# One block inversion emitted between dense projection tiles, and a full-width transpose in place of two narrow ones

## Chip, cores and metric

The kernel runs on one core of a Trainium2 chip. The metric is the device time of one execution in microseconds (us); several executions give a median. The trace was taken from one profiled execution of the kernel before the change.

## What is computed

One step of a one-layer hybrid decoder over 512 prompt tokens and 32 sample tokens: a half-step feed-forward, a projection of the normalised activations, two groups of heads (sparse attention and RWKV-7), an output projection and a second feed-forward.

```python
xp = ffn_half(xp, ffn1_norm[l], ffn1_wg[l], ffn1_wu[l], ffn1_wd[l])
zp = rms_norm(xp, mix_norm[l]) @ w_in[l]
...
o_nsa_p, wk_p, wv_p = nsa_prompt(qp, kvp, gp, cmp_w, rel_bias_table)
o_rw_p, wkv_p, sh_p = rwkv_mix(zp[..., NSA_COLS:], ...)
...
xp = xp + jnp.concatenate([o_nsa_p, o_rw_p], axis=-1) @ w_out[l]
xp = ffn_half(xp, ffn2_norm[l], ffn2_wg[l], ffn2_wu[l], ffn2_wd[l])
```

The RWKV group has 8 heads of width 64 and a delta-rule state. The kernel computes it in chunks of 64 tokens, and each chunk of each head needs the inverse of a 64x64 unit triangular matrix. That inverse is the place of the change.

## The kernel before, in words

Activations live transposed: 128 features on the partitions, 544 token columns as two halves of 272. The projection of the mixing stage, `w_in`, is cut into 25 tiles of 128 output features. A tile is eight feature blocks of the input by three products (high by high, high by low, low by high part) by two halves: 48 dense matmuls of 128x272 on TensorE (PE), all issued from line 159 (`dense`) into a PSUM tile `acc`, of which there are two. The weights of half a tile come with one DMA from SyncE (`wraw`), ScalarE (ACT) makes the high part (`wh`, line 150) and VectorE (DVE) the low part (`wl`, line 152).

Tiles 0 to 13 belong to RWKV: two for all heads, then three (key, value, receptance: `xs_k`, `xs_v`, `xs_r`) for each of four head pairs 0 to 3. So pair 2 has tiles 8 to 10 and pair 3 has tiles 11 to 13. `rwkv_prep(si)` works on half `si`, that is on pairs 2si and 2si+1; for each pair:

- `shifted` turns a projection tile into a token-shifted row block (DVE lines 483 to 491, GpSimd 487 to 489, ACT 490);
- two small matmuls for decay and in-context rate go through sigmoid on ACT (lines 562 to 565), a scan on DVE (566), a matmul by `blk1` for a norm (line 497, called from 569), then a chain of ACT (571, 572, 576, 580, 581) and DVE work (570, 574 to 591) that ends in the operands `bk` and `ar`;
- 64 block products of `bk` and `ar` (line 598) make the matrices `L` (DVE masks them at 601), 64x64 transposes by matmul (607, 614) give `BK` and `UV` (ACT 610, 617), and a last matmul by `blk1` (line 497 again) feeds `gbs` and `orw` (DVE 627 to 629). PE line 598 to this last matmul is called the tail of a pair below.

These small products rotate through two PSUM banks, `pp`; those of the inversion and of the chain of chunks through two others, `pq`.

`rwkv_inverse(L)` inverts the triangles of one half, so the first one covers pairs 0 and 1. It has two parts. The diagonal part runs on DVE: three transposes of `L` into `A` (lines 636, 638; the last two have 32 partitions each), an elimination of 15 steps with two instructions each (653, 654), and two transposes of the result, `Dt` and `Dn` (656, 658). The product part runs on PE in four groups of tiny matmuls, each of which needs an evacuation of the group ahead: 664 (64 products of 16 columns), then ACT 666; 672 and 674 (96 products), then DVE 677 and ACT 679; 685 (32 products), then ACT 688; 693 (32 products), then ACT 696. GpSimd copies blocks into `L` (668).

Instructions are written in program order, but a scheduler puts those of each engine into their final order, and each engine then works through its row strictly in order; with `keep_in_program_order` a matmul stays behind what was written ahead of it. Before the change no product of the inversion is held like that.

Of the kernel before, what the change touches and what calls it, by code (L numbers as in the profile page):

```python
# [7 lines left out]
F32 = mybir.dt.float32  # L8
F32R = mybir.dt.float32r
I32 = mybir.dt.int32  # L10
AF = mybir.ActivationFunctionType
# [6 lines left out]
KT = 8  # L18
# [10 lines left out]
HW = 272  # L29
# [19 lines left out]
class Step:  # L49
# [301 lines left out]
    def mix(self):  # L351
        nc = self.nc
        r = self.norm_end()
        with ExitStack() as st:
            self.mc = self.pool("mc", 1, st)
            self.un = self.pool("un", 1, st)
            self.orw = self.mc.tile([128, 4, 2, HW], F32, name="orw")
            un1 = self.un1 = self.pool("u1", 1, st)
            with ExitStack() as s0:
                un0 = self.pool("u0", 1, s0, side="right")  # L360
                with ExitStack() as s2:
                    self.rwkv_setup(s2)
                    self.lanes = "p"
                    S0 = self.rwkv_prep(0, r, un0)
                    self.lanes = "q"
                    self.rwkv_inverse(S0[0])
                    self.lanes = "p"
                    S1 = self.rwkv_prep(1, r, un1)
                    nc.scalar.dma_start(self.O["sh"], self.sho.rearrange("p a b -> p (a b)"))
                self.lanes = "q"  # L370
                self.ch = self.pool("ch", 1, s0, side="right")
                self.rwkv_chain(0, un0, *S0)
                self.rwkv_inverse(S1[0])
            self.az = self.pool("az", 1, st, side="right")
# [90 lines left out]
    def mix_consts(self):  # L465
# [10 lines left out]
        nc.gpsimd.tensor_copy(self.id2[64:128], self.ident[64:128, 64:128])  # L476

    def shifted(self, i, col, r, tp, xs):
        nc = self.nc
        p = self.win_tile(i)  # L480
        z = tp.tile([128, ZW], F32, name="zp", tag="zp", bufs=2)
# [46 lines left out]
    def rwkv_prep(self, si, r, up):  # L528
        nc, I = self.nc, self.I
# [14 lines left out]
        ar = []  # L544
        pcp = up.tile([128, 2, 8], F32, name="pcp")
        L = up.tile([128, 2, 16, 128], F32, name="L")
        BK = up.tile([128, 2, 2, 8, 64], F32, name="BK")
        UV = up.tile([128, 2, 2, 8, 64], F32, name="UV")
        for pi in range(2):
            p = 2 * si + pi  # L550
            if p == 1:
                room = self.un1.tile([128, 7, ZW], F32, name="prep", tag="L")
                k, v, rr, sig, a, Lc, sq = (room[:, j] for j in range(7))
# [38 lines left out]
            for h in range(2):  # L592
                pl = [self.ps() for hh in range(2)]
                for cc in range(4):
                    c = 4 * h + cc
# [33 lines left out]
            nc.vector.tensor_mul(c64(self.orw[:, p, 1, SW:HW]), half(pb[1][:, :ZW - ZP[1][0]]), half(v[:, ZP[1][0]:ZW]))  # L629
        return L, BK, UV, ar, pcp  # L630

    def rwkv_inverse(self, L):
        nc, un = self.nc, self.un
        A = un.tile([128, 32, 32], F32, name="ivA", tag="iA")
        Lt = L.rearrange("p x c t -> p t (x c)")
        nc.vector.transpose(A, Lt[:, 0:32])
        for s in (slice(32, 64), slice(96, 128)):
            nc.vector.transpose(A[s], Lt[s, 32:64])
        N = un.tile([128, 32, 32], F32, name="ivN", tag="iN")
# [17 lines left out]
        Dn = un.tile([128, 32, 32], F32, name="ivDn", tag="iD")  # L657
        nc.vector.transpose(Dn.rearrange("p b t -> p t b"), N)
        grp = [(hh, q, 64 * hh + 32 * q) for q in range(2) for hh in range(2)]
        T = un.tile([128, 16, 16], F32, name="ivT", tag="iN")  # L660
        p = self.ps()
        for c in range(16):
            for hh, q, g in grp:
                nc.tensor.matmul(p[g:g + 32, c * 16:c * 16 + 16], L[g:g + 16, hh, c, 32 * q:32 * q + 32], Dt[g:g + 16, 16 * hh + c, 0:16],
                                 start=True, stop=True)
        nc.scalar.activation(T, p[:, 0:256].rearrange("p (c s) -> p c s", s=16), AF.Copy, scale=self.half)
        for hh, q, g in grp:
            nc.gpsimd.tensor_copy(L[g:g + 32, hh, :, 32 * q:32 * q + 32], Dn[g:g + 32, 16 * hh:16 * hh + 16])
        pt, pz = self.ps(), self.ps()
        for c in range(16):  # L670
            for hh, q, g in grp[0:2]:
                nc.tensor.matmul(pt[g:g + 32, c * 16:c * 16 + 16], Dn[g:g + 32, 16 * hh + c], T[g:g + 32, c], start=True, stop=True)
            for hh, q, g in grp:
                nc.tensor.matmul(pz[g:g + 16, c * 16:c * 16 + 16], T[g:g + 32, c], Dn[g:g + 32, 16 * hh + c, 16:32], start=True, stop=True)
        for hh, q, g in grp[0:2]:
# [6 lines left out]
        for c in range(16):  # L682
            for hh in range(2):
                g = 64 * hh
                nc.tensor.matmul(p[g + 32:g + 64, c * 32:c * 32 + 32], L[g:g + 32, hh, c, 32:64], Dt[g:g + 32, 16 * hh + c], start=True, stop=True)
        for hh in range(2):
# [3 lines left out]
        for c in range(16):  # L690
            for hh in range(2):
                g = 64 * hh
                nc.tensor.matmul(p[g:g + 32, c * 32:c * 32 + 32], W[g + 32:g + 64, c], L[g + 32:g + 64, hh, c, 32:64], start=True, stop=True)
        for hh in range(2):
            s = slice(64 * hh, 64 * hh + 32)
            nc.scalar.activation(L[s, hh, :, 32:64], p[s].rearrange("p (c t) -> p c t", t=32), AF.Copy)

    def rwkv_chain(self, si, up, L, BK, UV, ar, pcp):
# [933 lines left out]
```

## Time and profile before

| | us |
|---|---|
| median of 3 runs | 1522.66 (1521.82 to 1527.6) |
| profiled execution, whole | 1521.93 |
| profiled execution, span from first to last instruction | 1520.1 |
| TensorE busy in the span | 1367.9 |
| VectorE, ScalarE, GpSimd busy | 707.0, 512.1, 250.7 |
| mean granted TensorE clock | 0.929 |

Times in the rows are counted from the start of the span. Busy time of an engine counts overlapping instructions once. A tiny or small matmul on 32-bit operands leaves two records in the trace, a dense one leaves one. The granted clock is 1.00 at 2.4 GHz and 0.50 at 1.2 GHz.

### The profile page before, as it was taken

To read this page: it belongs to the slowest core of one execution; us is meant where nothing else is said; L and a number is where in the kernel's file an instruction comes from. 1 tells how busy PE (TensorE), PEld (TensorE's weight loads), DVE (VectorE), ACT (ScalarE), POOL (GpSimd) and SP (SyncE) were. 2 spreads that over 40 slices of the span, in tenths; PEclk is the share of its full clock that TensorE was granted. 3 is DMA by queue.
4 is the path that set the end of the run, shared out by engine and by line. 5 is a ranking of instruction groups with operands and counts; after the bars stand their busy time and mean duration, and the time that the engine had idled before them with its cause. 6 is when DMAs were issued, how large, how long until landed. Compare 5 with 4: busy or idle time off the path is not lost.

```text
span 1520.1 us, 31735 instructions
## 1 busy us (share of the span) xinstructions
PE 1367.9 (90%) x13337; PEld 1272.0 (84%) x13337; DVE 707.0 (47%) x1357; ACT 512.1 (34%) x928; POOL 250.7 (16%) x313
## 2 busy tenths in 40 slices
PE   9969686877799999889899986889999999999996
PEld 8969586766799999778776884567999999999996
DVE  6423222222333345694968764457454444443223
ACT  6212121121232236545222334457443333332321
POOL 2153332415100011212000223320100000000100
PEclk9979697978799999997999997889999999999998
DMA  4533333434334342111131564731532222233332
GB/s 158 186 121 102 94 104 107 139 112 139 94 103 119 114 129 86 43 43 39 37 110 29 171 182 149 215 112 44 175 103 89 87 91 86 89 91 106 109 105 84
DMA packets 99329, 163.25 MB, mean 107 GB/s; under 512 B 16186, under 2 KB 42882, under 8 KB 98547
## 3 DMA queue, kind: packets, MB, share of 16 engines
q1 hardware_dynamic: 74978, 116.10, 25.0%
q0 software_dynamic: 9040, 25.24, 5.6%
q10 hardware_dynamic: 15168, 19.89, 4.4%
q8 instruction: 105, 1.72, 0.5%
q14 instruction: 38, 0.30, 0.1%
HBM read 150.19 MB, written 16.72 MB: 110 GB/s over the span
## 4 chain that ended last, share of the span: by engine, by line
PE 80%; issue 7%; DVE 6%; ACT 3%; another core or an unknown queue 1%; DMA 1%; POOL 0%; ACTq 0%; DVEq 0%; SPq 0%; POOLq 0%
PE acc L159 63%; PE pS L969 1%; PE pq L972 1%; PE po L969 1%; PE pp L969 1%; PE pq L714 1%; PE pq L956 1%; PE pp L956 1%; DMA wraw<-in_wg 1%; PE pp L598 1%; PE pp L796 1%; PE pp L497 1%; PE pp L159 1%; DVE ivt L653 0%
## 5 line engine op out<-in xcount | busy, mean ns | idle before, releaser
L159 PE MATMUL acc<-hl,wh 128*128 128x272 f32 x2064 | 437.9, 296 | 27.5 <-issue 26.4
L150 ACT ACTIVATE wh<-wraw 128x512 fp32r<-128x512 f32 x338 | 209.7, 620 | 685.6 <-PE acc L159 507.1
L159 PE MATMUL acc<-hh,wh 128*128 128x272 f32 x1808 | 394.9, 298 | 33.2 <-issue 29.9
L159 PE MATMUL acc<-hh,wl 128*128 128x272 f32 x1808 | 391.8, 297 | 26.0 <-issue 24.4
L152 DVE TENSOR_TENSOR wl<-wraw,wh 128x512 fp32r<-128x512 f32 x338 | 232.5, 688 | 337.4 <-ACT wh L150 279.7
L159 PEld LDWEIGHTS acc<-hl,wh 128*128 128x128 f32 x2064 | 332.0, 194 | 41.0 <-issue 37.2
L159 PEld LDWEIGHTS acc<-hh,wh 128*128 128x128 f32 x1808 | 296.0, 194 | 42.1 <-issue 35.6
L159 PEld LDWEIGHTS acc<-hh,wl 128*128 128x128 f32 x1808 | 293.2, 194 | 33.5 <-issue 30.5
L918 POOL DMA_INDIRECT cp<-in_cmp,idx x128 | 125.0, 976 | 204.6 <-PE pp L956 80.3
L159 PE MATMUL acc<-ah,wh 128*128 128x272 f32 x660 | 137.0, 289 | 0.0
L159 PE MATMUL acc<-al,wh 128*128 128x272 f32 x660 | 136.2, 287 | 0.0
L159 PE MATMUL acc<-ah,wl 128*128 128x272 f32 x660 | 135.5, 286 | 0.0
L126 POOL TENSOR_TENSOR ss<-ss,sq 128x544 f32<-128x544 f32 x23 | 32.0, 1393 | 599.7 <-ACT sq L122 584.3
L159 PEld LDWEIGHTS acc<-al,wh 128*128 128x128 f32 x660 | 104.0, 188 | 0.0
L159 PEld LDWEIGHTS acc<-ah,wl 128*128 128x128 f32 x660 | 103.3, 188 | 0.0
L159 PEld LDWEIGHTS acc<-ah,wh 128*128 128x128 f32 x660 | 102.9, 188 | 0.0
L194 DVE TENSOR_TENSOR t<-acc,r 128x544 f32<-128x544 f32 x42 | 30.4, 724 | 111.3 <-PE acc L159 87.3
L196 DVE TENSOR_TENSOR u<-acc,r 128x544 f32<-128x544 f32 x42 | 30.4, 724 | 108.8 <-PE acc L159 78.5
L918 POOL DMA_INDIRECT kv<-in_slc,idx x36 | 35.5, 986 | 130.1 <-DVE Y L747 64.2
L199 ACT ACTIVATE ah<-u 128x544 fp32r<-128x544 f32 x44 | 29.0, 658 | 65.1 <-DVE u L197 59.3
L200 DVE TENSOR_TENSOR al<-u,ah 128x544 fp32r<-128x544 f32 x44 | 31.9, 725 | 29.0 <-ACT ah L199 28.3
L1416 ACT ACTIVATE ra<-pq 128x512 f32<-128x512 f32 (+2 forms) x48 | 23.7, 521 | 35.9 <-remote 15.4
(515 smaller groups left out, 1482.0 us busy)
## 6 DMA issues: line engine op xcount, KB each, us to landing
wraw<-in_wg SPq DMA_DIRECT2D x88, 256.0 KB
wraw<-in_wu SPq DMA_DIRECT2D x88, 256.0 KB
wraw<-in_wd SPq DMA_DIRECT2D x80, 256.0 KB
wraw<-in_win SPq DMA_DIRECT2D x50, 256.0 KB
kv<-in_slc SPq DMA_DIRECT2D x60, 128.0 KB
x<-xr ACTq DMA_DIRECT2D x16, 272.0 KB
xr<-x ACTq DMA_DIRECT2D x16, 272.0 KB
wraw<-in_wout SPq DMA_DIRECT2D x16, 256.0 KB
```

The costliest lines, as they stand in the source:

```text
L126: nc.gpsimd.tensor_add(self.ss, self.ss, sq)
L150: nc.scalar.activation(wh[:, :m], w[:, :m], AF.Copy)
L152: nc.vector.tensor_sub(wl[:, :m], w[:, :m], wh[:, :m].bitcast(F32))
L159: self.nc.tensor.matmul(p[h] if isinstance(p, list) else p[:, h, :HW], a, b[:, h], start=f, stop=l)
L194: nc.vector.tensor_mul(t, pt, r)
L196: nc.vector.tensor_mul(u, pu, r)
L199: nc.scalar.activation(ah[:, f], u, AF.Copy)
L200: nc.vector.tensor_sub(al[:, f], u, ah[:, f].bitcast(F32))
L918: self.nc.gpsimd.indirect_dma_start(out=tile[:, k], out_offset=None, in_=rows, in_offset=bass.IndirectOffsetOnAxis(ap=self.idx[:, k0 + k:k ...
L956: nc.tensor.matmul(ph[64 * x:64 * x + 64, 0:w], self.w1[:, x, j], self.cp[:, 0:w // 4, x, j], start=j == 0, stop=j == 31)
L969: self.tc.keep_in_program_order(self.nc.tensor.matmul(*args, **kw))
L1416: self.nc.scalar.activation(t[:, 0:o + w], p[:, 0:o + w], AF.Copy)
```

## The change

The preparation of a half becomes a generator that stops after each pair. The first inversion is cut in two functions. `rwkv_diagonal` is written where the whole inversion stood, right after pair 1. `rwkv_inverse` is written after pair 2, and its four groups of products are now held in program order (`self.mm`), with pieces of tiles 11 and 12 between the groups: 20, 24 and 24 single dense matmuls, and the rest of the 96 behind the last group. The finished tiles are kept in `self.made` until pair 3 asks for them. The second inversion takes the same code with nothing to fill in. In the diagonal part the two 32-partition transposes become one of 128 partitions into a new tile `B`, from which ACT copies the two 32-partition slices that are wanted.

```diff
-                    S0 = self.rwkv_prep(0, r, un0)
+                    half0 = self.rwkv_prep(0, r, un0)
+                    next(half0)
+                    S0 = next(half0)
                     self.lanes = "q"
-                    self.rwkv_inverse(S0[0])
+                    diag = self.rwkv_diagonal(S0[0])
                     self.lanes = "p"
-                    S1 = self.rwkv_prep(1, r, un1)
+                    half1 = self.rwkv_prep(1, r, un1)
+                    next(half1)
+                    self.lanes = "q"
+                    self.rwkv_inverse(S0[0], diag, self.win_ahead(11, 12))
+                    self.lanes = "p"
+                    S1 = next(half1)
...
-                self.rwkv_inverse(S1[0])
+                self.rwkv_inverse(S1[0], self.rwkv_diagonal(S1[0]), iter(()))
...
+    def win_ahead(self, *tiles):
+        for i in tiles:
+            wt = self.wload(self.I["win"][i], KT)
+            p = self.made[i] = self.acc()
+            for k in range(KT):
+                xh, xl = self.hh[:, k], self.hl[:, k]
+                for a, b, f, l in ((wt[k][0], xh, k == 0, False), (wt[k][0], xl, False, False), (wt[k][1], xh, False, k == KT - 1)):
+                    for h in range(2):
+                        self.mm(p[:, h, :HW], a, b[:, h], start=f, stop=l)
+                        yield
...
-        p = self.win_tile(i)
+        p = self.made.pop(i) if i in self.made else self.win_tile(i)
...
-        return L, BK, UV, ar, pcp
+            yield L, BK, UV, ar, pcp
...
+        B = un.tile([128, 32, 32], F32, name="ivB", tag="iD")
+        nc.vector.transpose(B, Lt[:, 32:64])
         nc.vector.transpose(A, Lt[:, 0:32])
         for s in (slice(32, 64), slice(96, 128)):
-            nc.vector.transpose(A[s], Lt[s, 32:64])
+            nc.scalar.activation(A[s], B[s], AF.Copy)
...
+        return Dt, Dn
+
+    def rwkv_inverse(self, L, diag, ahead):
...
+        def fill(n):
+            for _ in range(n):
+                next(ahead, None)
...
-                nc.tensor.matmul(p[g:g + 32, c * 16:c * 16 + 16], L[g:g + 16, hh, c, 32 * q:32 * q + 32], Dt[g:g + 16, 16 * hh + c, 0:16],
+                self.mm(p[g:g + 32, c * 16:c * 16 + 16], L[g:g + 16, hh, c, 32 * q:32 * q + 32], Dt[g:g + 16, 16 * hh + c, 0:16],
...
+        fill(20)
...
+        fill(24)
...
+        fill(24)
...
+        fill(96)
```

Three places in the engines' rows show what moves. The first is PE at the norm of pair 2: `pp<-xs_wa` and `pp<-sq` are its small matmuls, `acc` rows are dense pieces, `ar,bk` are its block products. Before:

```order
L563 MATMUL pp<-xs_wa,w2a_5030 128x260
L497 MATMUL pp<-sq_6218,blk_5015 128x300
L159 MATMUL acc<-hh,wl 128x272
L497 MATMUL pp<-sq_6218,blk_5015 128x260
L159 MATMUL acc<-hh,wh 128x272 x2
L159 MATMUL acc<-hl,wh 128x272 x2
L159 MATMUL acc<-hh,wl 128x272 x2
```

With the change:

```order
L582 MATMUL pp<-xs_wa,w2a_5030 128x260
L516 MATMUL pp<-sq_5974,blk_5015 128x300
L516 MATMUL pp<-sq_5974,blk_5015 128x260
L617 MATMUL pp<-ar,bk_6216 64x128 x2
L617 MATMUL pp<-ar,bk_6217 64x128 x2
```

Before, 69 dense matmuls of tiles 11 and 12 follow the second norm matmul, and 18 stand ahead of it among the small ones; with the change there is none from the end of tile 10 to the end of pair 2's tail.

The second place is PE at the start of the first inversion's products (`pq<-ivDt,L` with 64 products is the first group). Before:

```order
L159 MATMUL acc<-hl,wh 128x272
L664 MATMUL pq<-ivDt,L 32x16 x64
L159 MATMUL acc<-hl,wh 128x272
L159 MATMUL acc<-hh,wl 128x272 x2
L159 MATMUL acc<-hh,wh 128x272 x2
L672 MATMUL pq<-ivT,ivDn 32x16 x2
L674 MATMUL pq<-ivDn,ivT 16x16 x4
```

With the change:

```order
L633 MATMUL pp<-ident,xs_v 64x64 x16
L516 MATMUL pp<-xs_r,blk_5015 128x300
L516 MATMUL pp<-xs_r,blk_5015 128x260
L1004 MATMUL pq<-ivDt,L 32x16 x64
L1004 MATMUL acc<-hh,wh 128x272 x2
L1004 MATMUL acc<-hl,wh 128x272 x2
L1004 MATMUL acc<-hh,wl 128x272 x2
```

The first group moved behind the whole tail of pair 2, which stood behind it and among the later groups before; behind it now come 20 dense pieces in place of 5, then 24 behind each of the next two groups and 76 (the end of tile 12 and all of tile 13) behind the last one.

The third place is ACT after pair 1's last evacuations (`BK`, `UV`). Before:

```order
L610 ACTIVATE BK<-pp 128x512 x2
L617 ACTIVATE UV<-pp 64x512 x2
L150 ACTIVATE wh<-wraw 128x512 x2
L564 ACT_TABLE_LOAD
L564 ACTIVATE sig<-pp,vec 128x300
```

With the change:

```order
L629 ACTIVATE BK<-pp 128x512 x2
L659 ACTIVATE ivA<-ivB 32x1024
L636 ACTIVATE UV<-pp 64x512 x2
L659 ACTIVATE ivA<-ivB 32x1024
L150 ACTIVATE wh<-wraw 128x512 x2
```

The two copies that take over from the narrow transposes stand ahead of and behind the evacuation of `UV`. On DVE the order round the elimination stays: the elimination, `Dt`, `Dn`, and only then `bk` and `ar` of pair 2.

## Rows read from the trace of the kernel before

**Rows 1.** The page: busy time of the engines, and the chain that ended last by engine (its first entries on one line).

```profile
PE 1367.9 (90%) x13337; PEld 1272.0 (84%) x13337; DVE 707.0 (47%) x1357; ACT 512.1 (34%) x928; POOL 250.7 (16%) x313
PE 80%; issue 7%; DVE 6%; ACT 3%; another core or an unknown queue 1%; DMA 1%; POOL 0%; ACTq 0%; DVEq 0%; SPq 0%; POOLq 0%
```

**Rows 2.** The timeline of PE from the end of tile 10 to pair 3's first small matmul: start, duration, line, operation, count of records, in brackets the idle time ahead and what ended it.

```profile
656.05 0.70 PE L497 MATMUL pp<-prep,blk 128*128 128x260 f32 x2
...
660.20 0.52 PE L562 MATMUL pp<-xs_wa,w2a 64*128 64x300 f32 x1
...
668.32 0.98 PE L497 MATMUL pp<-sq,blk 128*128 128x260 f32 x2 [1.05 <-ACT a L565]
...
680.51 1.26 PE L664 MATMUL pq<-ivDt,L 16*32 16x16 f32 x128 [1.27 <-DVE ivDt L656]
...
684.63 0.18 PE L674 MATMUL pq<-ivDn,ivT 32*16 32x16 f32 x1 [0.73 <-issue]
...
688.63 0.24 PE L674 MATMUL pq<-ivDn,ivT 32*16 32x16 f32 x5 [2.06 <-issue]
...
708.64 0.52 PE L562 MATMUL pp<-xs_wa,w2a 64*128 64x300 f32 x1
```

**Rows 3.** Busy time in two stretches, of the dense matmuls of line 159 alone: PE busy (records), weight loads, granted clock, DMA share, GB/s.

```profile
660.20:679.00 18.80, 13.51 (x88) 12.65 (x87) 0.91 0.14 43
679.00:708.64 29.64, 10.30 (x59) 8.48 (x58) 0.71 0.10 31
```

**Rows 4.** The timeline of DVE from the transposes of `L` to pair 2's operands.

```profile
652.28 1.98 DVE L636 STREAM_TRANSPOSE ivA<-L 128x1024 f32<-128x1024 f32 x1
...
654.87 4.03 DVE L638 STREAM_TRANSPOSE ivA<-L 32x1024 f32<-32x1024 f32 x2
...
659.37 0.15 DVE L653 TENSOR_TENSOR ivt<-ivN,ivA 128x2 f32<-128x2 f32 x1
659.44 0.42 DVE L629 TENSOR_TENSOR orw<-pp,prep 128x256 f32<-128x256 f32 x1
...
671.16 0.68 DVE L152 TENSOR_TENSOR wl<-wraw,wh 128x512 fp32r<-128x512 f32 x1
...
674.88 0.80 DVE L574 SCALAR_TENSOR_TENSOR sig<-xs_k,vec,sig 128x560 f32<-128x560 f32 x1 [0.27 <-ACT sig L572]
...
682.08 0.73 DVE L587 TENSOR_TENSOR bk<-a,sq 128x512 f32<-128x512 f32 x1
...
683.89 0.72 DVE L591 TENSOR_TENSOR ar<-xs_r,Lc 128x512 f32<-128x512 f32 x1
```

**Rows 5.** The timeline of ACT after pair 1's transposes, and the one group of ACT work on 1024 elements (groups by form: busy, mean ns).

```profile
654.80 1.20 ACT L617 ACTIVATE UV<-pp 64x512 f32<-64x512 f32 x2 [0.81 <-PE pp L614]
...
L756 ACT ACTIVATE gq<-Y 128x1024 f32<-128x1024 f32 x2 | 2.1, 1051 | 0.2 <-DVE Y L754 0.2
```

**Rows 6.** The timeline of PE over pair 3's tail, first and last row.

```profile
725.10 1.10 PE L598 MATMUL pp<-ar,bk 64*64 64x128 f32 x32 [1.22 <-DVE ar L591]
...
734.60 0.71 PE L497 MATMUL pp<-xs_r,blk 128*128 128x260 f32 x2
```

**Rows 7.** Groups by form on PE from 660.2 to 708.64 us: busy us, mean ns, then idle time ahead and its releaser.

```profile
L598 PE MATMUL pp<-ar,bk 64*64 64x128 f32 x64 | 4.2, 428 | 0.0
L674 PE MATMUL pq<-ivDn,ivT 32*16 32x16 f32 x128 | 3.1, 188 | 2.8 <-issue 2.8
...
L693 PE MATMUL pq<-L,ivW 32*32 32x32 f32 x64 | 2.2, 237 | 0.0
L685 PE MATMUL pq<-ivDt,L 32*32 32x32 f32 x64 | 1.9, 237 | 0.0
```

**Rows 8.** The timeline of PE: two dense pairs at each level of the clock.

```profile
670.00 0.66 PE L159 MATMUL acc<-hh,wl 128*128 128x272 f32 x2
670.46 0.66 PE L159 MATMUL acc<-hh,wh 128*128 128x272 f32 x2
...
676.19 0.41 PE L159 MATMUL acc<-hh,wl 128*128 128x272 f32 x2
676.44 0.41 PE L159 MATMUL acc<-hh,wh 128*128 128x272 f32 x2
```

**Rows 9.** Busy time of all engines in stretches: length, PE, weight loads, DVE, ACT, GpSimd, granted clock, DMA share, GB/s.

```profile
663.80:668.70 4.90, 2.23 (x10) 1.22 (x9) 4.80 (x12) 2.10 (x5) 0.50 (x3) 0.99 0.20 54
668.70:671.80 3.10, 3.10 (x14) 3.00 (x13) 3.10 (x8) 2.40 (x3) 0.00 (x0) 0.50 0.02 5
...
682.30:688.60 6.30, 3.39 (x190) 2.85 (x189) 5.71 (x12) 0.47 (x1) 5.94 (x6) 0.50 0.01 3
688.60:698.60 10.00, 9.97 (x204) 8.50 (x204) 3.42 (x6) 5.99 (x12) 1.64 (x4) 0.50 0.18 56
```

**Rows 10.** The second inversion: DVE's transposes, the ACT evacuations round them, and PE's wait behind them (timelines of DVE, ACT and PE).

```profile
732.28 3.96 DVE L638 STREAM_TRANSPOSE ivA<-L 32x1024 f32<-32x1024 f32 x2
...
738.53 1.08 ACT L721 ACTIVATE AT<-pq 128x512 f32<-128x512 f32 x2 [3.98 <-DVE ivN L654]
...
739.18 2.79 PE L714 MATMUL pq<-Y,L 64*64 64x64 f32 x64 [2.49 <-ACT AT L721]
```

**Rows 11.** The start of the attention, timeline of DVE, and the last stretch by busy time (columns as in rows 9).

```profile
917.14 0.69 DVE L1156 CUSTOM_DVE_ANT_1 S<-pp,mb 128x512 f32<-128x512 f32 x1 [8.03 <-remote]
...
1200.00:1520.00 320.00, 307.80 (x2449) 306.57 (x2447) 123.02 (x182) 95.23 (x151) 8.20 (x6) 0.99 0.31 95
```

More of the change, by code (lines that the diff above doesn't have):

```diff
@@ L353, in mix @@
         r = self.norm_end()
+        self.made = {}
         with ExitStack() as st:
@@ L629, in rwkv_prep, with rwkv_diagonal @@
             nc.vector.tensor_mul(c64(self.orw[:, p, 1, SW:HW]), half(pb[1][:, :ZW - ZP[1][0]]), half(v[:, ZP[1][0]:ZW]))
-        return L, BK, UV, ar, pcp
-    def rwkv_inverse(self, L):
+            yield L, BK, UV, ar, pcp
+    def rwkv_diagonal(self, L):
         nc, un = self.nc, self.un
@@ L658, in rwkv_inverse @@
         nc.vector.transpose(Dn.rearrange("p b t -> p t b"), N)
+        return Dt, Dn
+    def rwkv_inverse(self, L, diag, ahead):
+        nc, un = self.nc, self.un
+        Dt, Dn = diag
+        def fill(n):
+            for _ in range(n):
+                next(ahead, None)
         grp = [(hh, q, 64 * hh + 32 * q) for q in range(2) for hh in range(2)]
@@ L671, in rwkv_inverse @@
             for hh, q, g in grp[0:2]:
-                nc.tensor.matmul(pt[g:g + 32, c * 16:c * 16 + 16], Dn[g:g + 32, 16 * hh + c], T[g:g + 32, c], start=True, stop=True)
+                self.mm(pt[g:g + 32, c * 16:c * 16 + 16], Dn[g:g + 32, 16 * hh + c], T[g:g + 32, c], start=True, stop=True)
             for hh, q, g in grp:
-                nc.tensor.matmul(pz[g:g + 16, c * 16:c * 16 + 16], T[g:g + 32, c], Dn[g:g + 32, 16 * hh + c, 16:32], start=True, stop=True)
+                self.mm(pz[g:g + 16, c * 16:c * 16 + 16], T[g:g + 32, c], Dn[g:g + 32, 16 * hh + c, 16:32], start=True, stop=True)
+        fill(24)
         for hh, q, g in grp[0:2]:
@@ L684, in rwkv_inverse @@
                 g = 64 * hh
-                nc.tensor.matmul(p[g + 32:g + 64, c * 32:c * 32 + 32], L[g:g + 32, hh, c, 32:64], Dt[g:g + 32, 16 * hh + c], start=True, stop=True)
+                self.mm(p[g + 32:g + 64, c * 32:c * 32 + 32], L[g:g + 32, hh, c, 32:64], Dt[g:g + 32, 16 * hh + c], start=True, stop=True)
+        fill(24)
         for hh in range(2):
@@ L692, in rwkv_inverse @@
                 g = 64 * hh
-                nc.tensor.matmul(p[g:g + 32, c * 32:c * 32 + 32], W[g + 32:g + 64, c], L[g + 32:g + 64, hh, c, 32:64], start=True, stop=True)
+                self.mm(p[g:g + 32, c * 32:c * 32 + 32], W[g + 32:g + 64, c], L[g + 32:g + 64, hh, c, 32:64], start=True, stop=True)
         for hh in range(2):
```

## Prediction

> **What bounds the kernel now.** I read the page first: PE is busy for 90% of the span and makes up 80% of the chain that ended last [rows 1]. So the time is the length of PE's row, and a change pays only if it takes idle time or slow-clock time out of that row. Next I walked PE's timeline over the stretch that the change touches, from the end of tile 10 (pair 2's first small matmul, 660.20) to the same matmul of pair 3 (708.64): 48.44 us [rows 2]. In it lie exactly tiles 11 to 13, 3 x 48 = 144 dense matmuls, most of them (x88) ahead of 679 and x59 behind (the three over 144 belong to tile 10's end and the edges) [rows 3].
>
> Three things are lost there. PE waits 1.27 us for the inversion's `Dt`, 0.73 and 2.06 us inside the groups 672 and 674 without a shown cause, 1.05 us for pair 2's sigmoids [rows 2]. And the clock is at half (0.50) from 668.7 to 671.8 and from 682.3 to 698.6 [rows 9]. A dense pair starts every 0.25 us at the full clock and every 0.46 us at half [rows 8]. This is what the change is after.
>
> The third view is DVE's timeline, and it tells what the 88 dense matmuls are good for. From 659.37 to 682.08 DVE works without a break worth naming at the elimination and its transposes, mixed with pair 2's preparation; only then come `bk` and `ar`, done at 683.89 + 0.72 = 684.6 [rows 4]. For 24 us pair 2 can give PE next to nothing. Tiles 11 and 12 are what PE does meanwhile.
>
> **The change, part by part.** The order shows that with the change no dense matmul is left between the end of tile 10 and the end of pair 2's tail; the first inversion group stands behind that tail as well, although `Dt` is ready earlier. The cover of DVE's 24 us is moved away, and it is spent later, on waits of 4 us. I walk PE's row again with the new order.
>
> Start. DVE saves one of three transposes: 1.98 + 4.03 become two of 1.98 [rows 4]. But ACT now copies two slices of 1024 elements, about 1.05 us each by the only such group [rows 5], one ahead of `UV` and one behind. The first can start when `A` is transposed, 652.28 + 2 x 1.98 = 656.2; then `UV` 1.2 us [rows 5], then the second copy: 656.2 + 1.05 + 1.2 + 1.05 = 659.5. So the elimination starts no earlier than now (659.37), say 659.7. And pair 1's last norm matmul, which needs the bank that `UV` leaves, moves from 656.05 [rows 2] to about 658.5; tile 10 ends 2.3 us later. That delay is covered, because of what follows.
>
> Wait for `ar`. DVE's row loses one `wl` (0.60 to the next start), one `orw` that now lies ahead (0.33) and a wait of 0.27 [rows 4]: 1.2 us. So `ar` is done at 684.6 + 0.3 - 1.2 = 683.7. Until then PE has six small matmuls and stands idle for some 19 us; this was 13.5 us of dense work [rows 3].
>
> Tail of pair 2. Pair 3's tail in this trace took from 725.10 to 734.60 + 0.71 = 735.3, which is 10.2 us [rows 6]; it goes hand in hand with DVE and ACT, so the dense pieces in it are hardly on the path. After 19 us of idleness the clock will be at half; the block products of pair 2 at half took 4.2 us [rows 7] against 1.1 us for half of them in pair 3 [rows 6], of which I charge 1.0, since the rest falls on DVE waits. The tail ends at 683.7 + 11.2 = 694.9.
>
> Inversion and tiles 11 to 13. Tiny products: 1.26 [rows 2] + 3.1 + 1.9 + 2.2 [rows 7] = 8.5 us. Dense: 144 x 0.125 = 18.0 us at the full clock. The evacuations between the groups are covered by 20 or 24 pieces each (2.5 to 5.5 us), as is meant; I leave 1 us for the waits without a cause (bounds 0 and 2.8). The clock term has no row of the same mixture. Nearest from below: after the dense work resumed at 668.7 the clock was back within 3.1 us [rows 9], a loss of 1.6 us. Nearest from above: through waits and tiny groups it stayed at half for 16.3 us [rows 9]; all 68 pieces of the three fills at half cost 8.5 us more, all 144 pieces 18. I take two fills, 44 pieces, 5.5 us, because 20 pieces last 4.6 us at half and a tiny group of 3.1 us follows at once. Sum 8.5 + 18.0 + 1.0 + 5.5 = 33.0, and the stretch ends at 727.9 in place of 708.64: **+19.3 us**.
>
> By the Trainium skill, TensorE: Matmul & The Clock Gate, section "Why this matters for your kernels", the engine keeps its high clock as long as matmuls follow each other without gaps. That speaks for the pieces between the groups: if they held the clock up all along, the clock term would be 0 and the sum 13.8 us. By that rule it also speaks against the change, whose longest gap lies ahead of the pieces; the trace agrees with this side, since the clock fell behind the stretch from 663.8 to 668.7 in which PE was busy for 2.23 of 4.90 us [rows 9].
>
> Second inversion. It has nothing to fill in. The transposes end 2 us earlier (they end at 736.24 now [rows 10]), but `UV` and with it the last `orw` wait for ACT's first copy, and `AT`, for which PE stood 2.49 us [rows 10], waits for that `orw`: 734.2 + 1.05 + 1.2 + 0.7 + 0.5 = 737.7 in place of 738.5. So -0.5 us, bounds -2 and +2, since the scheduler also shuffles pieces of later tiles there. GpSimd's and SyncE's rows lose nothing and gain nothing here: the same loads in almost the same order, and PE waits for none of them.
>
> Later stages. The second feed-forward is PE-bound (307.8 of 320 us [rows 11]) and starts that much later. **Forecast:** 1521.93 + 19.3 - 0.5 = 1540.7; the profiled execution lies 0.7 us under the median, so **1541 us**, 1.2% slower.
>
> **Rivals.** *The cover is not missed (faster).* If the rows above are wrong about DVE, because `ar` of pair 2 comes 15 us earlier, the new order costs nothing ahead of the inversion, and it wins the waits of 1.27 + 0.73 + 2.06 us and half of the 16.3 us at the low clock, 8 us: about 1510. It decides at whether PE's idle time ahead of `ar,bk` is under some 4 us. Against it stands that the elimination keeps its place ahead of `bk` in DVE's row: 5%.
>
> *The delay is swallowed later (no change).* At the start of the attention DVE, and PE behind it, wait 8.03 us for an event outside the engines [rows 11]. If that event has a fixed time, 8 us of the shift vanish there. With the lowest shift of the sum (683.7 + 10.2 + 7.4 + 18.0 + 1.6 = 720.9, so +12.2) this gives +4, about 1526. Against it: no row gives the event a clock of its own, and all work ahead of it shifts. 9%.
>
> *The clock does not come back (slower still).* All 144 pieces at half, and a tail without a hidden part: +18 - 5.5 + 2 on the forecast, 1555. It takes that the alternation of tiny and dense keeps the clock low, which the stretch from 682.3 to 698.6 hints at with few dense pieces in it. 6%.
>
> **How the numbers follow.** The forecast has the remaining 80%; its own range is +12.2 - 2 to +25 + 2 (8.5 of clock, 2.8 of waits, 1 more in the tail), 1533 to 1550. The range for 8 in 10 stretches a little to both sides: 1529 to 1552. About 0.5%, 7.6 us, is what a measurement of this kernel can tell from no change, so the border is at 1530.3. The forecast and the slow-clock rival are slower (86%), the swallowed delay is within (9%), the rival that wins is faster (5%).
>
> **What would show it.** In the changed profile PE should have a wait of about 15 us, released by DVE's `ar` (line 610), and the stretch from tile 10's end to pair 3's first small matmul should be 17 us or so longer than 48.4, plus 2.3 that tile 10 ends later. The elimination should start within 1 us of 659.4, not 2 us earlier. Between the four groups of products PE should not wait. The granted clock should be 0.50 from about 665 into the second fill. A dense stretch ahead of `ar,bk`, or a shift at 860 us that is half of that at 727, would prove me wrong.

## The result, and the profile after

| | before | changed |
|---|---|---|
| median of 4 runs, us | 1523.03 (1521.82 to 1527.60) | 1543.57 (1537.27 to 1545.32) |
| profiled execution: span | 1520.1 | 1543.5 |
| mean granted TensorE clock | 0.929 | 0.918 |

The ratio is 1.0122 [1.0086, 1.0157]: 1.2% slower. The page of the changed kernel, the lines that answer to [rows 1]:

```profile
PE 1373.3 (89%) x13337; PEld 1280.3 (83%) x13337; DVE 700.7 (45%) x1355; ACT 518.8 (34%) x933; POOL 247.7 (16%) x313
PE 77%; issue 9%; DVE 7%; ACT 3%; DMA 2%; POOL 1%; another core or an unknown queue 0%; ACTq 0%; DVEq 0%; SPq 0%; POOLq 0%
```

The same number of matmuls, 5.4 us more of PE busy time, and 23.4 us more span: the loss is mostly time in which PE stands. By the medians the loss is 20.5 us, so this pair of traces shows some 3 us more than the usual loss. The timeline of PE from pair 1's last norm matmul to pair 3's block products, to be laid beside [rows 2] and [rows 6] (a pair has 32 block products, not 64, with two records each, so a row `ar,bk` of x32 is half of a pair's):

```profile
658.55 0.68 PE L516 MATMUL pp<-prep,blk 128*128 128x260 f32 x2 [0.94 <-DVE orw L647]
...
662.54 0.52 PE L581 MATMUL pp<-xs_wa,w2a 64*128 64x300 f32 x1
...
684.63 1.99 PE L617 MATMUL pp<-ar,bk 64*64 64x128 f32 x32 [16.38 <-DVE ar L610]
687.42 2.57 PE L617 MATMUL pp<-ar,bk 64*64 64x128 f32 x32 [0.80 <-DVE L L620]
690.78 2.67 PE L626 MATMUL pp<-ident,bk 64*64 64x64 f32 x64 [0.80 <-DVE L L620]
694.15 1.97 PE L633 MATMUL pp<-ident,xs_v 64*64 64x64 f32 x32 [0.70 <-ACT BK L629]
696.05 2.60 PE L516 MATMUL pp<-xs_r,blk 128*128 128x300 f32 x4
698.58 1.91 PE L1004 MATMUL pq<-ivDt,L 16*32 16x16 f32 x128
...
710.55 1.20 PE L1004 MATMUL pq<-ivDt,L 32*32 32x32 f32 x64
...
714.89 1.20 PE L1004 MATMUL pq<-L,ivW 32*32 32x32 f32 x64
...
725.75 0.52 PE L581 MATMUL pp<-xs_wa,w2a 64*128 64x300 f32 x1
...
742.26 1.10 PE L617 MATMUL pp<-ar,bk 64*64 64x128 f32 x32 [1.22 <-DVE ar L610]
```

One wait of 16.38 us, released by DVE's `ar`, stands where 88 dense matmuls stood before. Behind 698.58 the plan works as written: no group of products waits for its evacuation. The busy time by stretch (columns as in [rows 9]):

```profile
668.70:684.00 15.30, 0.00 (x0) 0.00 (x0) 15.13 (x23) 6.04 (x8) 1.30 (x7) 0.60 0.00 0
684.00:700.00 16.00, 13.08 (x270) 10.44 (x274) 5.01 (x10) 2.27 (x4) 0.00 (x0) 0.50 0.01 2
700.00:705.00 5.00, 5.00 (x57) 4.96 (x49) 0.00 (x0) 0.47 (x1) 2.44 (x4) 0.50 0.01 3
705.00:710.00 5.00, 5.00 (x215) 4.72 (x214) 1.00 (x3) 2.14 (x5) 0.00 (x0) 0.92 0.01 3
```

PE does nothing for 15.3 us while DVE works for 15.13 of them; the clock falls to half in this stretch (a mean of 0.60) and stays there to about 706. DVE's and ACT's timelines round the transposes (before: [rows 4, 5]):

```profile
653.56 2.00 DVE L656 STREAM_TRANSPOSE ivB<-L 128x1024 f32<-128x1024 f32 x1
655.48 1.92 DVE L657 STREAM_TRANSPOSE ivA<-L 128x1024 f32<-128x1024 f32 x1
...
660.82 0.16 DVE L674 TENSOR_TENSOR ivt<-ivN,ivA 128x2 f32<-128x2 f32 x1 [1.12 <-ACT ivA L659]
...
683.91 0.67 DVE L610 TENSOR_TENSOR ar<-xs_r,Lc 128x512 f32<-128x512 f32 x1
```

```profile
657.44 1.06 ACT L659 ACTIVATE ivA<-ivB 32x1024 f32<-32x1024 f32 x1 [2.17 <-DVE ivA L657]
658.51 1.20 ACT L636 ACTIVATE UV<-pp 64x512 f32<-64x512 f32 x2
659.73 1.06 ACT L659 ACTIVATE ivA<-ivB 32x1024 f32<-32x1024 f32 x1
```

The transposes take 3.92 in place of 6.01 us, and the elimination starts 7.26 us behind their start, against 7.09 before: it waits for ACT's second copy.

Now the sum. Let **S** be the time from the first transpose of the first inversion (DVE) to pair 3's first block product (PE `ar,bk`). Before it is 652.28 to 725.10 = 72.82 [rows 4, 6], changed 653.56 to 742.26 = 88.70: +15.9. The 1.28 ahead of S come before anything that the change touches. What is left, 6.2 us, lies behind pair 3. Two places there catch the eye. The first is the second inversion, on PE's timeline, before and changed:

```profile
790.09 0.19 PE L674 MATMUL pq<-ivDn,ivT 32*16 32x16 f32 x2 [0.95 <-issue]
...
793.82 1.92 PE L796 MATMUL pp<-S,ars 64*32 64x512 f32 x4 [0.66 <-issue]
```

```profile
807.12 0.20 PE L1004 MATMUL pq<-ivT,ivDn 32*32 32x16 f32 x2 [0.94 <-issue]
...
810.85 0.21 PE L1004 MATMUL pq<-ivDn,ivT 32*16 32x16 f32 x2 [2.25 <-issue]
```

PE stands 0.94 + 2.25 = 3.2 us inside one group of products, between the matmuls of the sample rows (`S,ars`), against 0.95 + 0.66 = 1.6 before; the profile names no releaser ("issue"). The other is the block compression. First the changed kernel's PE there, then two stretches of the kernel before and of the changed one: from pair 3's first block product to the first small product of the block compression (`px,w1r`), and from there to the first `w,hid` product behind it. The last row is the part of the changed kernel's second stretch with the lowest clock:

```profile
891.53 0.36 PE L1293 MATMUL pp<-px,w1r 128*64 128x16 f32 x6 [0.44 <-issue]
892.32 0.64 PE L1293 MATMUL pp<-px,w1r 128*64 128x16 f32 x15 [0.42 <-issue]
```

```profile
725.10:870.19 145.09, 138.73 (x2333) 107.46 (x2333) 111.17 (x220) 36.10 (x66) 7.62 (x12) 0.95 0.27 86
870.19:902.74 32.55, 28.83 (x294) 26.79 (x293) 24.36 (x58) 13.64 (x25) 8.32 (x9) 0.90 0.64 171
```

```profile
742.26:887.20 144.94, 136.46 (x2348) 108.58 (x2348) 110.36 (x222) 42.64 (x74) 8.24 (x12) 0.96 0.29 91
887.20:927.39 40.19, 36.12 (x301) 33.56 (x300) 24.20 (x60) 11.26 (x22) 8.53 (x9) 0.75 0.48 140
892.00:910.00 18.00, 17.11 (x101) 16.39 (x102) 7.00 (x19) 2.03 (x6) 4.00 (x5) 0.54 0.47 140
```

The first stretch, with the second inversion in it, is as long as before (144.94 and 145.09 us), so its longer waits cost nothing on balance. The second takes 7.6 us more, at a mean clock of 0.75 in place of 0.90; over 18 us of it the clock is 0.54 while PE is busy for 17.11. A part comes back at the start of the attention, where DVE's wait for the event outside the engines falls from 8.03 us [rows 11] to 5.45:

```profile
938.23 0.69 DVE L1191 CUSTOM_DVE_ANT_1 S<-pp,mb 128x512 f32<-128x512 f32 x1 [5.45 <-remote]
```

### The profile page after: what moved, and what is told of

The parts are those of the page before. It is cut to its first block, busy times and chain, and to the rows that moved or that the text cites. A ratio compares the mean times of both kernels' runs of the same rounds, so it can differ in the third digit from the quotient of the medians.

```text
span 1543.5 us, 31747 instructions
## 1 busy us (share of the span) xinstructions
PE 1373.3 (89%) x13337; PEld 1280.3 (83%) x13337; DVE 700.7 (45%) x1355; ACT 518.8 (34%) x933; POOL 247.7 (16%) x313
## 4 chain that ended last, share of the span: by engine, by line
PE 77%; issue 9%; DVE 7%; ACT 3%; DMA 2%; POOL 1%; another core or an unknown queue 0%; ACTq 0%; DVEq 0%; SPq 0%; POOLq 0%
PE acc L159 60%; PE po L1004 2%; PE pp L1004 1%; PE pS L1004 1%; PE pq L1007 1%; PE pq L991 1%; PE acc L1004 1%; PE pq L1004 1%; PE pq L749 1%; PE pp L991 1%; PE pp L617 1%; DVE ivt L674 1%; DMA wraw<-in_wg 1%; PE pp L159 1%; DMA tbd<-tbl 1%
## 5 line engine op out<-in xcount | busy, mean ns | idle before, releaser
L159 PE MATMUL acc<-hl,wh 128*128 128x272 f32 x2032 | 427.6, 295 | 27.6 <-issue 26.3
L159 PE MATMUL acc<-hh,wl 128*128 128x272 f32 x1776 | 386.5, 297 | 32.3 <-issue 28.6
L159 PE MATMUL acc<-hh,wh 128*128 128x272 f32 x1776 | 388.8, 298 | 29.0 <-issue 27.6
L159 PEld LDWEIGHTS acc<-hl,wh 128*128 128x128 f32 x2032 | 326.8, 194 | 38.1 <-issue 34.5
L159 PEld LDWEIGHTS acc<-hh,wl 128*128 128x128 f32 x1776 | 289.4, 195 | 39.0 <-issue 33.7
L159 PEld LDWEIGHTS acc<-hh,wh 128*128 128x128 f32 x1776 | 291.1, 195 | 36.6 <-issue 32.5
```

Source lines behind the costliest of these rows:

```text
L159: self.nc.tensor.matmul(p[h] if isinstance(p, list) else p[:, h, :HW], a, b[:, h], start=f, stop=l)
```

## The experiments

**Theory (cover):** the loss is the dense work that was taken out from under DVE's elimination. **Rivals:** the transposes and ACT's copies (*transposes*); the products held behind pair 2's tail (*place*); the clock after the idle time (*clock*); later, for the 6 us behind pair 3, *order* against *scatter*.

The experiments ran on chips where the kernel before takes 1364 to 1367 us, and they are compared with it there. What is shorter there is the front (the transposes start at 533 to 537 us) and the part behind pair 3 (755.5 us in e6, 795.0 in the first trace), not S. The column of S and of the waits is read from one trace each; medians and ratios are over all executions, but for one of e4. No trace of the kernel before was taken there; e6 stands in for it (S 72.84).

| | S, us | PE waits for `Dt`, then for `ar,bk` of pair 2 | median over before, us | ratio |
|---|---|---|---|---|
| e1 both wide transposes only | 73.33 | 3.89 / none | +8.5 | 1.0061 [1.0039, 1.0084] |
| e2 changed, narrow transposes | 88.84 | none / 14.04 | +14.1 | 1.0100 [1.0066, 1.0134] |
| e3 changed, no pieces | 76.36 | none / 7.23 | +9.9 | 1.0071 [1.0040, 1.0101] |
| e4 pieces of tile 13 alone | 73.73 | 3.78 / 1.59 | +0.9 | 1.0012 [0.9988, 1.0035] |
| e5 changed again | 86.10 | none / 14.67 | +19.9 | 1.0133 [1.0102, 1.0164] |
| e6 wide, first inversion only | 72.84 | 3.89 / none | -1.5 | 0.9987 [0.9966, 1.0007] |
| e7 wide, second inversion only | 73.27 | 0.89 / none | +6.0 | 1.0054 [1.0028, 1.0080] |
| e8 changed, clock held | 85.45 | none / 0.80 | +23.4 | 1.0172 [1.0143, 1.0201] |
| e9 tile 13, wide in first only | 70.81 | 3.76 / 1.57 | +7.9 | 1.0046 [1.0017, 1.0075] |
| e10 tile 13, narrow | 73.02 | none / 2.85 | +5.5 | 1.0019 [0.9994, 1.0044] |
| e11 pieces of tiles 12 and 13 | 78.10 | 9.53 / 0.38 | +10.6 | 1.0073 [1.0049, 1.0098] |
| e12 changed, wide in first only | 86.15 | none / 14.69 | +16.2 | 1.0117 [1.0081, 1.0154] |

**e1.** The kernel before with this:

```diff
-            nc.vector.transpose(A[s], Lt[s, 32:64])
+            nc.scalar.activation(A[s], B[s], AF.Copy)   # B: one transpose of 128 partitions
```

> The kernel before with the transpose part alone (one wide transpose and two ACT copies for the two narrow transposes). Theory, cover: this part is worth nothing either way; the saved 2 us of DVE wait for ACT's copies, the elimination starts within 1 us of where it did, and the time is 1521 to 1526. Rival, transposes: ACT's copies ahead of and behind UV hold up DVE and pair 1's last norm matmul so much that they make up a good part of the loss: 1530 or more. Second rival, the saving counts: 1520 or less.

The theory missed: +8.5 us lies where the rival had it (1530 or more is +7 and over). But the rival's mechanism isn't there: S is 73.33, half a microsecond from before, so the first inversion is innocent. The loss lies behind pair 3, which neither foresaw; e5 to e7 take this up.

**e2.** The changed kernel with the line of e1 the other way round.

> The changed kernel with the two narrow transposes put back, all else as changed. Theory, cover: the PE wait ahead of pair 2's block products stays at 15 to 18 us, and the time stays at 1541 to 1546. Rival, transposes: 1536 or less.

The wait stays (PE):

```profile
566.86 1.98 PE L617 MATMUL pp<-ar,bk 64*64 64x128 f32 x32 [14.04 <-DVE ar L610]
```

The time, +14.1, missed both: the theory had 18 to 23 us over the kernel before, the rival 13 or less, and the wait was to be 15 to 18 us. But S is as long as in the changed kernel, 88.84, so a loss of this size stands without any wide transpose. The time lies 5.9 us under the changed kernel (e5) with overlapping intervals; the trace is of the longest run, 1385.67 us, and doesn't show where that difference lies.

**e3.**

```diff
-                    self.rwkv_inverse(S0[0], diag, self.win_ahead(11, 12))
+                    self.rwkv_inverse(S0[0], diag, iter(()))
```

> The changed kernel with no pieces between the first inversion's groups: the products stay held and stay written behind pair 2, but tiles 11 to 13 are written as before and are free to go ahead. Theory, cover: tiles 11 and 12 come back under DVE's elimination, the wait ahead of pair 2's block products falls from 16.4 to under 4 us, and the time is 1524 (1519 to 1531), a little over the kernel before because the inversion stands behind the tail of pair 2. Rival, place: the held products behind the tail cost most of the loss, and the time is 1536 or more.

S falls by about 10 us to 76.36. The wait falls to 7.23, not under 4:

```profile
567.97 1.99 PE L617 MATMUL pp<-ar,bk 64*64 64x128 f32 x32 [7.23 <-DVE ar L610]
```

So the place has a price too, some 3.5 us of S: the first group of products no longer stands in this gap (in e4, where it does, 3.78 + 1.90 + 1.59 = 7.27 us stand there). The larger part is the cover. The time itself, +9.9, was over the forecast's range by 2 us and short of the rival; some 6 of it lie outside S, as in e1, which has both wide transposes like this one.

**e4.** Tiles 11 and 12 are written ahead of the inversion and free to move, tile 13 alone is cut in pieces:

```diff
             self.shifted(3 + 3 * p, 3 + 3 * p, r, tp, v)
+            if p == 3:
+                yield
...
                     next(half1)
+                    next(half1)
...
-                    self.rwkv_inverse(S0[0], diag, self.win_ahead(11, 12))
+                    self.rwkv_inverse(S0[0], diag, self.win_ahead(13))
```

> The changed kernel with pieces of tile 13 alone between the groups (48 in place of 96); the row blocks of tiles 11 and 12 are written ahead of the inversion and are free to go ahead. Theory, cover: 78 dense matmuls stand under the elimination again, the wait ahead of pair 2's block products is under 4 us, the pieces still cover the evacuations, and the time is 1521 (1515 to 1528), no more than the kernel before. Rival, place: products held behind the tail cost by themselves, 1536 or more. If the clock stays at half through the tail all the same, 1528 to 1533.

The trace is of its longest run, 1383.72 us, which the median leaves out, so only S and the waits are read from it (e9's trace has the same waits, 3.76 and 1.57):

```profile
563.22 1.90 PE L1007 MATMUL pq<-ivDt,L 16*32 16x16 f32 x128 [3.78 <-DVE ivDt L680]
...
566.70 1.98 PE L620 MATMUL pp<-ar,bk 64*64 64x128 f32 x32 [1.59 <-DVE ar L613]
```

With 78 dense matmuls back between pair 2's last norm matmul and its block products the wait ahead of `ar,bk` is 1.59 us, and the kernel is as fast as before, with the held groups and the pieces still in it. One more thing came back: the first group of products stands ahead of pair 2's tail again, and only the other three behind it, so e4 gives back the cover and a part of the place together. By e3 the cover is the larger part; e11 and e8 below bear it out. Against the kernel before, the pieces do no harm and bring nothing that can be measured.

**e5.** The changed kernel unaltered.

> The changed kernel unaltered, beside the kernels of this call, since the chip of the first four experiments is faster at the front than the one of the first timing. Theory: 15.9 us from the projection stretch by the cover that is gone, 6 to 8 us from a second low-clock stretch at the small products of the block compression, together 20 to 25 us over the kernel before. Rival: the downstream part was scatter of the one profiled run, 14 to 17 us over the kernel before.

+19.9, at the lower edge of the theory's range: S gives 13.3 over e6. S is 2.6 us shorter than in the first trace because the clock came back some 14 us after `ar,bk` (at about 582), not 21. A row of PE and two stretches of e5:

```profile
581.92 1.26 PE L1004 MATMUL pq<-ivDt,L 16*32 16x16 f32 x128
```

```profile
581.00:582.00 1.00, 1.00 (x10) 0.34 (x14) 0.33 (x1) 0.00 (x0) 0.00 (x0) 0.57 0.00 0
582.00:584.00 2.00, 2.00 (x135) 1.97 (x136) 0.43 (x1) 0.47 (x1) 0.72 (x2) 1.00 0.04 8
```

The same rows take more or less with the point at which it rises. In e12 it also rose some 14 us after `ar,bk` and S is 86.15, in e2 some 21 and S is 88.84.

**e6 and e7.** A flag in the diagonal part takes the lines of e1 in one of the two inversions:

```diff
+        if self.firstinv:            # e7: if not self.firstinv
...                                  # wide transpose and two copies
+        else:
...                                  # two narrow transposes
```

> The kernel before with the wide transpose and its copies in the first inversion alone. The order of the products between the block compression and the attention is that of the kernel before. Theory, order: the 8 us that the transpose part cost everywhere come from the second inversion, which shifts the later order; here within 2 us of the kernel before. Rival, transposes: the copies of the first inversion cost, 5 us or more over the kernel before.

> The kernel before with the wide transpose and its copies in the second inversion alone. The order of the products between the block compression and the attention is that of the changed kernel. Theory, order: 6 to 10 us over the kernel before, with PE at half clock for some 16 us from the small products of the block compression on. Rival, transposes of the first inversion: within 2 us of the kernel before.

Both came as the theory *order* had it: -1.5 and +6.0 us, intervals apart. The place of the low clock did not: e7's long stretch at half clock lies behind the second inversion, not at the block compression. PE in the second inversion, and the 24 us from 64 us behind pair 3's block products on, e6 first:

```profile
671.60 0.19 PE L682 MATMUL pq<-ivDn,ivT 32*16 32x16 f32 x2 [0.77 <-issue]
```

```profile
671.79:695.79 24.00, 23.80 (x494) 13.53 (x483) 16.00 (x34) 6.67 (x13) 0.00 (x0) 0.79 0.01 3
```

and e7:

```profile
672.17 0.17 PE L682 MATMUL pq<-ivDn,ivT 32*16 32x16 f32 x1 [1.41 <-issue]
675.63 0.21 PE L682 MATMUL pq<-ivDn,ivT 32*16 32x16 f32 x3 [2.04 <-issue]
```

```profile
670.79:694.79 24.00, 20.58 (x364) 11.52 (x365) 11.36 (x19) 4.44 (x9) 1.00 (x2) 0.64 0.01 2
```

PE is busy for 20.58 of 24 us at a clock of 0.64, against 23.80 at 0.79. With the wide transpose in its second inversion the scheduler puts five of the sixteen `S,ars` matmuls of e7 ahead of the second inversion's first group, where one stands in e6, and the order stays another from there into the attention; e1 and the changed kernel have it too. The wait itself, 1.41 + 2.04 in place of 0.77 us, lies inside the group of 96 products that stands together in both orders, and the profile shows no cause for it. It doesn't hang on this order: with the order of e6 in that place e9 waits 0.83 + 2.65 us there, the kernel before 1.6.

**e8.** PE is given something to do in the wait:

```diff
+            if p == 2:
+                pw = self.acc()
+                for _ in range(116):
+                    self.mm(pw[:, 0, :HW], self.hh[:, 0, 0, 0:128], self.hh[:, 1, 0], start=True, stop=True)
             for h in range(2):
                 pl = [self.ps() for hh in range(2)]
```

> The changed kernel with 116 more dense matmuls, whose results nobody reads, ahead of pair 2's block products; they take about 14.5 us at the full clock, less than PE's wait for DVE there. Theory, clock: the products of pair 2 start when they did, but the tail takes 10 to 11.5 us in place of 13.95 and the first 20 pieces 2.5 in place of 4.8, so the stretch to pair 3's first small matmul is 4 to 7 us shorter and the time 4 to 7 us under the changed kernel. Rival: the tail goes by DVE and ACT and the clock costs only the pieces: 2.5 us or less.

The trace is of its shortest run, 1379.75 us, 10 us under the median, so only the stretch is read from it. The wait is gone and the clock was up when `ar,bk` began:

```profile
565.17 1.10 PE L621 MATMUL pp<-ar,bk 64*64 64x128 f32 x32 [0.80 <-DVE ar L610]
```

```profile
549.50:563.00 13.50, 13.50 (x104) 13.50 (x103) 13.33 (x19) 5.34 (x7) 1.31 (x7) 0.95 0.00 0
563.00:567.00 4.00, 2.48 (x43) 2.01 (x42) 3.69 (x8) 0.00 (x0) 0.00 (x0) 1.00 0.01 4
567.00:576.00 9.00, 7.44 (x129) 6.74 (x130) 1.91 (x4) 1.41 (x3) 0.00 (x0) 0.55 0.00 0
576.00:580.00 4.00, 3.96 (x137) 2.33 (x137) 0.95 (x3) 1.33 (x3) 0.60 (x1) 0.74 0.02 4
```

Then the tail lost it by itself: 0.55 between 567 and 576, with PE busy for 7.44 of 9 us. The tail took 12.92 us (565.17 to 578.09) against 13.95, and S is 0.65 us less than in e5 and 3.25 less than in the first trace of the changed kernel, where the theory had 4 to 7. The median is no lower than that of the changed kernel; the intervals overlap, and why it is rather higher, outside the stretch, stays open. So the theory *clock* isn't borne out, nor is the thought that the gap costs by PE's idleness alone: the gap is full of work, the clock is up, and S is 85.45 all the same, since the work is not that of tiles 11 and 12.

**e9 and e10.** e4 with the flag of e6, and e4 with narrow transposes throughout.

> Tile 13 alone as pieces (as in the fourth experiment), with the wide transpose in the first inversion only. Theory, cover in both inversions: the second inversion gets back the products of the sample rows (S by ars, 4 of 16) between its groups, the 6 us that its wide transpose costs go, and the time is 4 to 8 us under the fourth experiment's ratio, that is 0 to 7 us under the kernel before (1359 to 1366). Rival: pair 3's operands come from DVE as late as ever, what PE gains it waits out there, and the time is within 2 us of the kernel before.

> Tile 13 alone as pieces, narrow transposes in both inversions as in the kernel before. Theory: the first inversion's wide transpose is worth nothing either way, so within 2 us of the run with the wide one in the first inversion alone. Rival: the wide transpose saves its 2 us of DVE once PE's cover is in place, 3 us or more over that run.

e9's theory, a gain, was wrong, and so was its rival: it has the shortest S of all, 70.81, and is 7.9 us slower than before: from pair 3's block products to the end of the span its trace takes 1369.2 - 605.12 = 764.1 us, e6's takes 1363.3 - 607.79 = 755.5. Its order behind the second inversion is again another than that of before (a gate matmul, `sg,g`, among the small products of the block compression, 62 dense matmuls in place of 54 ahead of the next transposes), though no transpose there is wide. So the wide transpose is one way to shift the later order, not the only one, and the expectation that the sample products between the groups decide is not borne out. e10 came 2.4 us under e9 with overlapping intervals, close to its theory (within 2 us) and against its rival (3 us or more over). Its difference of medians, 5.5 us, and its ratio, 2.6 us, part; the interval holds 1. And with tile 13 alone as pieces the wide transpose of the second inversion costs nothing: e4 has it, e10 has none, and their ratios are 1.0012 and 1.0019.

**e11.** As e4, with the stop behind tile 11 and `win_ahead(12, 13)`.

> The changed kernel with tile 11 free to go ahead and tiles 12 and 13 kept as pieces: 48 dense matmuls more under the elimination than in the changed kernel, 48 fewer than in the fourth experiment. Theory, cover: each tile kept back costs its 48 x 0.125 = 6 us of cover, so the wait ahead of pair 2's block products is 8 to 11 us, the stretch to pair 3's first small matmul 5 to 8 us longer than in the fourth experiment, and the time 6 to 13 us over the kernel before (1372 to 1380). Rival: one tile is cover enough, 3 us or less over the fourth experiment.

```profile
561.76 1.90 PE L1007 MATMUL pq<-ivDt,L 16*32 16x16 f32 x128 [9.53 <-DVE ivDt L680]
565.24 1.99 PE L620 MATMUL pp<-ar,bk 64*64 64x128 f32 x32 [0.38 <-DVE ar L613]
```

One more tile kept back, 9.53 in place of 3.78 us ahead of `Dt`: 5.75 us, close to the theory's 48 x 0.125 = 6. The theory had this wait ahead of `ar,bk`, where 0.38 us are left: the first group stands ahead of the tail here, as in e4, so these two runs differ in the cover and hardly in the place. One tile stands behind the elimination in e4, two here, all three in the changed kernel: S is 73.73, 78.10 and 86.10, the time +0.9, +10.6 and +19.9 us.

**e12.** The changed kernel with the flag of e6.

> The changed kernel with the wide transpose in the first inversion only; the second has its narrow transposes back, and from the sample products on PE's order is that of the kernel before. Theory, order behind the second inversion: 5 to 8 us under the changed kernel, that is 12 to 15 us over the kernel before (ratio 1.009 to 1.011), with PE waiting 1 us or less among the second inversion's products in place of 3.2; the 13 to 16 us of the first inversion stay. Rival, scatter of the low clock: no steady difference from the changed kernel, 18 us or more over the kernel before.

+16.2, 3.8 us under e5, just outside the forecast and with overlapping intervals. Its trace has the order of before behind the second inversion and a wait of 1.27 us there (1 or less was expected):

```profile
685.92 0.21 PE L1010 MATMUL pq<-ivDn,ivT 32*16 32x16 f32 x2 [1.27 <-issue]
```

## Why the prediction came out, step by step

The forecast was 1541, the median is 1543.57, for the reason given: PE has nothing to do while DVE eliminates. The first rival (cover not missed) had its condition, an idle time under 4 us, refuted at 16.38. The second (swallowed at the attention) happened to a small part: the wait there fell by 2.6 us, but the shift had grown ahead of it. The third (clock never back) is refuted by 0.92 from 705 on. But three sizes were off: the tail, the inversion with its tiles, and what lies behind the second inversion. They cancelled for the most part; that the sum came within 3 us is in part luck. Measured times less the 1.28 us by which this trace was late beforehand:

| step | forecast | measured |
|---|---|---|
| elimination starts | 659.7 | 659.5 |
| tile 10 ends later by | 2.3 | 1.1 |
| `ar` of pair 2 done | 683.7 | 683.3 |
| tail of pair 2 | 11.2 | 13.95 |
| inversion and tiles 11 to 13 | 33.0 | 27.2 |
| shift at pair 3's first small matmul | +19.3 | +15.8 |
| pair 3's block products to the block compression, with the second inversion | -0.5 | -0.15 |
| everything behind | 0 | +6.4 |

- *Start and `ar`.* Right within 0.4 us. ACT's copies eat what DVE's transpose saved, as the rows of ACT foretold; e6 shows that the pair is worth nothing measurable in the first inversion.
- *Tail.* "It goes hand in hand with DVE and ACT, so the dense pieces in it are hardly on the path": true of the pieces, but the half clock was charged 1.0 us and cost more. The three matmul groups at 690.78, 694.15 and 696.05 alone take 2.67, 1.97 and 2.60 us. What the prediction took its size from, pair 3's tail before the change, had dense pieces in every wait and the full clock:

```profile
725.00:735.30 10.30, 10.18 (x189) 8.94 (x190) 9.02 (x11) 2.79 (x5) 0.16 (x1) 1.00 0.08 27
```

Without the pieces the tail ran at 0.50, and in e8 it lost the clock though it began with it. With free dense matmuls back in it, the tail of pair 2 took 11.0 us in e3, where the clock was back after 3 us of it, and 15.2 us in e4's trace, where it stayed at 0.50 for 12: dense work in the tail doesn't settle the clock by itself, and the clock decides some 4 us of the tail.
- *Inversion and tiles.* The tiny groups were sized from rows at half clock (3.1, 1.9, 2.2); at the full clock they took 2.1 (705.25 to 707.34), 1.2 and 1.2. The waits without a cause were 0, not 1.0, and the clock cost some 2.8 us, not 5.5: one fill at half, not two, since the clock was back at about 706, ahead of the second fill. By [rows 8] a piece takes 0.23 us at half and 0.125 at full, so even two fills (44 pieces) make 4.6 us and not 5.5.
- *Second inversion.* Right in this trace: -0.15 us against -0.5.
- *Later stages.* The step that failed. "Starts that much later" put everything behind the second inversion at nothing, and the scheduler's shuffling of later pieces was taken for small change. The block compression took 7.6 us more, at a clock of 0.75 in place of 0.90, and 1.3 us came back by the output projection. In the experiments this stretch (`px,w1r` to `w,hid`) goes with its clock: 28.1 to 28.6 us at 1.00 (e2, e6, e12), 29.7 at 0.94 (e7), 33.0 at 0.89 (e5), 39.1 at 0.74 (e1). From the output projection on every trace takes 460.0 to 460.2 us.
- *What moves the clock there.* e6 against e7 (7.5 us, intervals apart) shows that the wide transpose of the second inversion costs in the kernel before, by what stands behind it. e2 and e12 lie under e5 (5.9 and 3.8 us), but their intervals overlap with its own, and with tile 13 alone as pieces the wide transpose costs nothing (e4 and e10). So the order behind pair 3 bears on the loss, but doesn't fix it: e5 and e7 have the same order of PE there, and e7 loses most ahead of the block compression (148.85 us from pair 3's block products, e6 143.50), e5 inside it. Why the clock falls at one place or the other stays open.

By the Trainium skill, TensorE: Matmul & The Clock Gate, section "Why this matters for your kernels", idle gaps cost the engine its high clock. The first trace of the changed kernel agrees: the clock fell in the gap of 16.38 us. e8's trace agrees only in part: filling the long gap held the clock up to 567, and it fell in the tail, where no wait ahead of a matmul was over 0.80 us.

No version beats the kernel before: e6 (0.9987 [0.9966, 1.0007]) and e4 (1.0012 [0.9988, 1.0035]) are no different from it.

## What to carry to other kernels

Before moving dense work into a gap, look at what it covers where it stands now: here 4 us of waits were bought with 16 us of cover. Dense work is worth most under the longest chain of another engine, and it can be spent only once. And where a scheduler sets the order, an edit that saves a few microseconds on a side engine may reorder stages that it doesn't touch; compare the order of everything behind it, and test each place of an edit by itself.

## What was not expected of the hardware

- The clock falls without a long gap: in e8 to 0.55 over 9 us in which PE was busy 7.44 us with small products and waits of 0.80; in the changed kernel at the block compression after waits of 0.42 and 0.44 us.
- Its return differs between two traces of the changed kernel in the same order of work, one from where the kernel before takes 1523 us and one from where it takes 1367: about 21 us behind `ar,bk` in the first, about 14 us in e5, 2.6 us of S.
- Holding PE busy through a wait of 14.7 us took 0.65 us off S against e5 and 3.25 against the first trace, and nothing off the median.
- Small groups at half clock and at full: 1.91 and 1.26 us for the 64 products of 16 columns (698.58 here, 581.92 in e5).
